# A macaron block on one core: load order of the head, state-space tables a group ahead, a higher step rate, and the last product by token halves

## The chip, the cores and the metric

The kernel runs on one core of one Trainium2 chip. The metric is device time in microseconds (us). One execution is profiled by the hardware: its span runs from the first to the last instruction of the core. TensorE is called PE in the profile, VectorE is DVE, ScalarE is ACT, GpSimd is POOL and SyncE is SP.

## The reference

One block over 256 tokens of width 2048, all in float32:

```
h = rms_norm(x);  x = x + 0.5 * (silu(h @ w_gate) * (h @ w_up)) @ w_down       # FFN1, width 5632
h = rms_norm(x);  proj = h @ w_in                                              # 1024 + 2048 columns
y_a = s5_mixer(proj[:, :1024])        # diagonal complex state space: 64 groups of 16 channels, 64 states,
                                      # x_t = a x_(t-1) + b u_t, y = gelu(Re(c x) + d u); y * sigmoid(y @ w_glu + b)
y_b = sgu_mixer(proj[:, 1024:])       # u, v = gelu halves; v = layer_norm(v); u * (w_s (masked) @ v + b_s)
g_a, g_b = sigmoid(h @ w_gate2 + b)
x = x + (g_a * (y_a @ w_branch_a) + g_b * (y_b @ w_branch_b)) @ w_out
h = rms_norm(x);  x = x + 0.5 * (silu(h @ w_gate) * (h @ w_up)) @ w_down       # FFN2
return rms_norm(x)
```

## The kernel before, in words

**Products.** Every float32 operand is split into a high part (rounded to the type fp32r) and a low part, and each product is three matmuls into one PSUM accumulator: high by high (L216), weights' low part (L217), activations' low part (L218). The tokens lie in two halves of 128 (h = 0, 1), and a matmul has 512 output columns. One `step` is one k-tile of 128 by 512 columns for both halves, six matmuls.

**Weights.** They stream through SP's DMA queue in chunks of 1 MB, 128 x 2048, that is four k-steps (24 matmuls). ScalarE makes the high part of a chunk (`whi`, L148), VectorE then the low part (`wlo`, L149). There are three raw buffers and three pairs of split buffers, and a chunk is split two chunks ahead (LOOK = 2): the split of chunk c+2 is issued at the start of chunk c and can start once chunk c-1 has been used.

**Order of the work.** The kernel writes the order of every engine's instructions by hand. `take` hands out a k-step of weights, and calls `tick` before it. A tick runs, in this order: work that was put off to this tick (`at`), evacuations of finished accumulators (`pend`), at a chunk's start the split of the chunk after next, and then steps of a filler. A filler is a generator (`s5_prepare`, `layer_norm`, `sgu`, `s5_mix`); each `yield` ends one of its steps, and each tick adds a rate (`credit[1]`: 0.3 to 0.35 in FFN1, 0.5 in the mixer) of a step. A `yield` with no work before it is a pause. `drain` runs all that is left of the fillers at once.

**Stages.** FFN1 runs in groups of 4, 4 and 3 column blocks of its hidden width, the first of them with gate and up in one pass (`begin`). In it the filler `s5_prepare` computes the tables of the state-space part and writes them to DRAM: for four groups each of `vt` (L532 to L543, from `eb` and `bt`), of `ca`, `bb` and a 64 x 64 matrix (L544 to L591, from `par`) and of `tab` (L592 to L612). Then come w_in's six jobs (v, v, ub, ub, and the two of u_a, whose evacuation writes t (L891), transposes it (L258, four transposes to a tile) and copies it to `u_all` (L883)), four pairs of a gate g_b and a branch product, three jobs of g_a, the glu product, the last g_a, the branch a, w_out, and FFN2. `sgu` (L852) runs beside the u_a jobs; `s5_mix` starts two ticks after them and is drained by `split_y` eight ticks into the third g_a job; `split_y` splits `yT` into `ysp`, which the glu product (L232) reads.

**The state-space filler.** `s5_mix` treats four groups of 8 channel pairs one after another. In each, two products with `vt` (L662) go to PSUM, VectorE rotates them by `tab` (L639), scans them (L681), rotates back into `xs`, and products with `tmat` (L698) and `cm` (L701) give y, which goes to DRAM (L713) and back in another layout (L714) on POOL's queue. `tab` and `d4` come in one buffer each, as do `tmat` and `cm`; the loads stand at the start of the group (L645 to L653).

**PSUM.** Six banks hold accumulators (three of `acc`). Two banks (pool `ms`, L91) serve all transposes, sgu products and state-space products in turn; such a tile is named q.

**The head.** Twenty small matmuls on `ident` run first. SP loads `vec_sb`, the first two tiles of the transposed input `xT`, the first chunk in four pieces, and then chunks and the rest of `xT`. `x_sb`, the input in its own layout (2 MB), is loaded through POOL's queue (L778) at tick 8, which the order of POOL places ahead of any wait.

**The end.** `down_out` runs the four column blocks m of FFN2's last group (12 k-steps, three chunks each). After the last, both halves are added to x, squared, multiplied by the norm's gain, scaled by the norm's root and stored: four pieces of 128 x 1024 on VectorE and ScalarE, 512 KB each.

## Time and profile before

| | |
|---|---|
| median of 3 runs | 2087.6 us (2086.0 to 2088.61) |
| profiled execution, device time | 2085.11 us |
| its span | 2083.3 us, 23136 instructions |
| mean granted TensorE clock | 0.991 |
| DMA | 412.20 MB, mean 198 GB/s |
| weight splits | 359 chunks; ScalarE 1.90 us, VectorE 2.27 us each (means) |

A chunk's 24 matmuls take 5.45 us, so a k-step takes 1.36. Rows of the windows table give the length of a stretch, then for PE, PEld (TensorE's weight loads), DVE, ACT and POOL the busy time and the number of instructions, then the TensorE clock granted by the throttle (1.00 is full), the share of the 16 DMA engines and GB/s. Rows of the waits give what waited and for what, then the total in us, the count and the longest. Rows of the timeline begin with the start and the length, both in us; the bracket at the end holds the engine's idle time before it and what ended it. Rows of DMA issues end with the size of one and the us from issue to landing.

### The profile page before, as it was taken

To read this page: it belongs to the slowest core of one execution; us is meant where nothing else is said; L and a number is where in the kernel's file an instruction comes from. 1 tells how busy PE (TensorE), PEld (TensorE's weight loads), DVE (VectorE), ACT (ScalarE), POOL (GpSimd) and SP (SyncE) were. 2 spreads that over 40 slices of the span, in tenths; PEclk is the share of its full clock that TensorE was granted. 3 is DMA by queue.
4 is the path that set the end of the run, shared out by engine and by line. 5 is a ranking of instruction groups with operands and counts; after the bars stand their busy time and mean duration, and the time that the engine had idled before them with its cause. 6 is when DMAs were issued, how large, how long until landed. Compare 5 with 4: busy or idle time off the path is not lost. (4 is left out here: it accounts for less than half of the span.)

```text
span 2083.3 us, 23136 instructions
## 1 busy us (share of the span) xinstructions
PE 2034.3 (98%) x9764; PEld 1681.5 (81%) x9764; DVE 1126.6 (54%) x1095; ACT 862.8 (41%) x702; POOL 73.0 (4%) x135
## 2 busy tenths in 40 slices
PE   8999999999999999999989899999999999999997
PEld 6888888887888888878777788888888888888886
DVE  4765665546664555556555665554454444544454
ACT  5543344443334454443333544443433334333443
POOL 0000001111000000011100000000000000000000
PEclk9999999999999999999999999999999999999999
DMA  7457766555655455566555455555555555555553
GB/s 305 182 197 240 244 222 210 190 201 180 221 204 195 171 191 213 191 236 211 200 200 188 170 182 182 202 198 186 191 193 191 193 184 187 194 199 185 189 180 117
DMA packets 65769, 412.20 MB, mean 198 GB/s; under 512 B 10192, under 2 KB 10592, under 8 KB 19840
## 3 DMA queue, kind: packets, MB, share of 16 engines
q1 hardware_dynamic: 52848, 376.49, 50.6%
q0 software_dynamic: 10800, 30.03, 4.5%
q10 hardware_dynamic: 2016, 4.20, 0.6%
q8 instruction: 76, 1.25, 0.2%
q14 instruction: 29, 0.24, 0.0%
HBM read 398.21 MB, written 12.45 MB: 197 GB/s over the span
## 5 line engine op out<-in xcount | busy, mean ns | idle before, releaser
L149 DVE TENSOR_TENSOR wlo<-raw,whi 128x2048 fp32r<-128x2048 f32 (+1 forms) x359 | 815.8, 2274 | 789.3 <-ACT whi L148 789.2
L148 ACT ACTIVATE whi<-raw 128x2048 fp32r<-128x2048 f32 (+1 forms) x359 | 681.5, 1901 | 907.1 <-PE acc L218 832.0
L216 PE MATMUL acc<-whi,h 128*128 128x512 f32 x1856 | 728.7, 393 | 5.9 <-ACT whi L148 5.9
L217 PE MATMUL acc<-wlo,h 128*128 128x512 f32 x1856 | 724.8, 391 | 4.8 <-DVE wlo L149 4.8
L218 PE MATMUL acc<-whi,h 128*128 128x512 f32 x1856 | 724.2, 390 | 0.0
L216 PEld LDWEIGHTS acc<-whi,h 128*128 128x128 f32 x1856 | 349.7, 188 | 79.5 <-ACT whi L148 7.0
L217 PEld LDWEIGHTS acc<-wlo,h 128*128 128x128 f32 x1856 | 349.7, 188 | 78.0 <-DVE wlo L149 6.7
L218 PEld LDWEIGHTS acc<-whi,h 128*128 128x128 f32 x1856 | 349.6, 188 | 73.2
L216 PE MATMUL acc<-whi,gt 128*128 128x512 f32 x704 | 276.0, 392 | 0.0
L218 PE MATMUL acc<-whi,gt 128*128 128x512 f32 x704 | 276.0, 392 | 0.0
L217 PE MATMUL acc<-wlo,gt 128*128 128x512 f32 x704 | 275.1, 391 | 0.0
L217 PEld LDWEIGHTS acc<-wlo,gt 128*128 128x128 f32 x704 | 132.5, 188 | 28.7
L218 PEld LDWEIGHTS acc<-whi,gt 128*128 128x128 f32 x704 | 132.6, 188 | 28.0
L216 PEld LDWEIGHTS acc<-whi,gt 128*128 128x128 f32 x704 | 132.6, 188 | 27.9
L318 ACT ACTIVATE t<-acc,rc 128x512 f32<-128x512 f32 x44 | 27.9, 686 | 69.4 <-PE acc L218 69.4
L216 PE MATMUL acc<-whi,mT 128*128 128x512 f32 x128 | 50.2, 392 | 0.0
L218 PE MATMUL acc<-whi,mT 128*128 128x512 f32 x128 | 49.8, 389 | 0.0
L217 PE MATMUL acc<-wlo,mT 128*128 128x512 f32 x128 | 49.8, 389 | 0.0
L293 DVE SCALAR_TENSOR_TENSOR x_sb<-acc,x_sb 128x1024 f32<-128x1024 f32 x27 | 33.1, 1225 | 27.6 <-PE acc L218 27.6
L273 ACT ACTIVATE junk<-x_sb 128x512 bf16<-128x512 f32 x32 | 20.2, 631 | 64.6 <-DVE x_sb L293 53.0
L328 DVE SCALAR_TENSOR_TENSOR t<-acc,rc,t 128x512 f32<-128x512 f32 x44 | 31.0, 746 | 21.7 <-PE acc L218 21.6
L244 ACT ACTIVATE gt<-q 128x512 fp32r<-128x512 f32 x44 | 23.9, 596 | 31.3 <-PE q L258 31.3
(195 smaller groups left out, 1031.2 us busy)
## 6 DMA issues: line engine op xcount, KB each, us to landing
raw<-in_w1d_dram SPq DMA_DIRECT2D x44, 1024.0 KB, 4.9
raw<-in_w2g_dram SPq DMA_DIRECT2D x44, 1024.0 KB, 4.8
raw<-in_w2u_dram SPq DMA_DIRECT2D x44, 1024.0 KB, 4.8
raw<-in_w2d_dram SPq DMA_DIRECT2D x44, 1024.0 KB, 4.8
raw<-in_w1g_dram SPq DMA_DIRECT2D x40, 1024.0 KB, 4.9
raw<-in_w1u_dram SPq DMA_DIRECT2D x40, 1024.0 KB, 4.9
raw<-in_w_in_dram SPq DMA_DIRECT2D x24, 1024.0 KB, 4.8
raw<-in_w_gb_dram SPq DMA_DIRECT2D x16, 1024.0 KB, 4.9
```

Of the source, the lines that this page charges most:

```text
L148: act.activation(out=hi[:, s], in_=r[:, s], func=AF.Copy)
L149: dve.tensor_tensor(out=lo[:, s], in0=r[:, s], in1=f(hi[:, s]), op=ALU.subtract)
L216: pe.matmul(acc[:, h, :], lhsT=lhs[:, k, 0, t], rhs=hi, start=first, stop=False)
L217: pe.matmul(acc[:, h, :], lhsT=lhs[:, k, 0, t], rhs=lo, start=False, stop=False)
L218: pe.matmul(acc[:, h, :], lhsT=lhs[:, k, 1, t], rhs=hi, start=False, stop=last)
L244: act.activation(out=dst[:, :, 0, :], in_=src, func=AF.Copy)
L273: act.activation(out=j, in_=x_sb[:, h, m * N:m * N + N], func=AF.Square, accum_out=ssq[:, h, m:m + 1])
L293: dve.scalar_tensor_tensor(out=xs, in0=acc, scalar=scale, in1=xs, op0=ALU.mult, op1=ALU.add)
L318: act.activation(out=s[:, h, :], in_=acc[:, h, :], func=AF.Silu, scale=rc(h))
L328: dve.scalar_tensor_tensor(out=s[:, h, :], in0=acc[:, h, :], scalar=rc(h), in1=s[:, h, :], op0=ALU.mult, op1=ALU.mult)
```

## The change

It has six parts. (1) In the head, `vec_sb` is loaded through ScalarE's queue; the first tile of `xT` goes alone ahead of the first piece of the first chunk, and the second tile behind that piece; `x_sb` is loaded through SP's queue between chunks, at tick 8. (2) In `s5_prepare`, `par` has two buffers and is loaded a group ahead, with its three pauses once and not per group; two more pauses stand between the load of `eb` and `bt` and their use. (3) In `s5_mix`, `tab` and `d4` of the next group are loaded after the last use of those of this group, `tmat` and `cm` after the products that read them; both stand ahead of y's transfers on POOL's queue; two more pauses precede the products. (4) Once `s5_mix` starts, the rate is 0.68 and not 0.5. (5) `sgu` has two more pauses ahead of its transposes. (6) In the last product all twelve k-steps are taken first, and then all matmuls of half 0 run, and all of half 1; each half has an epilogue of its own, in four pieces of 512 columns, with stores of 256 KB.

```diff
-    def rms():
-        r = ev.tile([P, 2], F32, tag="rc", name="rc", bufs=2)
+    def rms(hs=slice(0, 2)):
+        r = ev.tile([P, 2], F32, tag="rc", name="rc", bufs=2)[:, hs]
         s = small()
-        dve.tensor_reduce(out=s[:, 0:2], in_=ssq, axis=AX.X, op=ALU.add)
-        rsqrt(r, s[:, 0:2], D, s[:, 2:4])
+        n = hs.stop - hs.start
+        dve.tensor_reduce(out=s[:, 0:n], in_=ssq[:, hs, :], axis=AX.X, op=ALU.add)
+        rsqrt(r, s[:, 0:n], D, s[:, 2:2 + n])
...
+        def load_par(g):
+            t = pb.tile([P, 4, GP, 16], F32, tag="par", name="par", bufs=2)
+            pool.dma_start(out=t, in_=s5bc[:, :, g * GP:(g + 1) * GP, :])
+            return t
...
             yield
             yield
             yield
+            yield
+            yield
             vt = pb.tile([P, 2, GP * 64], F32, tag="p2", name="vt")
...
+        parn = load_par(0)
+        yield
+        yield
+        yield
         for g in range(NG):
             gs = slice(g * GP, (g + 1) * GP)
-            par = pb.tile([P, 4, GP, 16], F32, tag="p0", name="par")
-            pool.dma_start(out=par, in_=s5bc[:, :, gs, :])
-            yield
-            yield
-            yield
+            par = parn
+            if g + 1 < NG:
+                parn = load_par(g + 1)
...
+        def load_tab(g):
+            t = sp.tile([P, 2, GP, 64], F32, tag="tab", name="tab")
+            pool.dma_start(out=t.rearrange("p i q j -> p (i q j)"), in_=stash_w[g])
+            d = sp.tile([P, GP, 64], F32, tag="d4", name="d4")
+            act.activation(out=d, in_=rho4[:, g * GP:(g + 1) * GP].unsqueeze(2).to_broadcast([P, GP, 64]),
+                           func=AF.Copy)
+            pool.memset(d[:, :, 0:1], 0.0)
+            return t, d
+
+        def load_cm(g):
...
             o_(mt[3], mt[1], co, ALU.mult)
             o_(xs[:, 1, :, 1:65], mt[2], mt[3], ALU.add)
+            if g + 1 < NG:
+                tab, d4 = load_tab(g + 1)
+            yield
+            yield
             yield
             yield
             q = ms.tile([P, 512], F32, tag="ms", name="q")
...
+            if g + 1 < NG:
+                tmat, cm = load_cm(g + 1)
             yield
...
-    nc.sync.dma_start(out=vec_sb, in_=vec)
-    nc.sync.dma_start(out=xT[:, 0:2, :], in_=xt[:, 0:2, :])
+    act.dma_start(out=vec_sb, in_=vec)
+    nc.sync.dma_start(out=xT[:, 0:1, :], in_=xt[:, 0:1, :])
...
-    at(8, lambda: pool.dma_start(out=x_sb, in_=xk))
+    at(8, lambda: nc.sync.dma_start(out=x_sb, in_=xk))
...
             yield
             yield
+            yield
+            yield
             turned(ub, c * N, lambda b, q, c=c: split2(ybT[:, 4 * c + 2 * b:4 * c + 2 * b + 2], q))
...
+        credit[1] = 0.68
         fillers.append(s5_mix(sp, u_all))
...
-        for k in range(kt):
-            step(acc, gt, k, k == 0, k == kt - 1)
-        s = slice(3 * N, 4 * N)
+        pieces = [take(N) for _ in range(kt)]
+        c3 = slice(3 * N, 4 * N)
         for h in range(2):
-            xs = x_sb[:, h, s]
+            t = slice(h * P, h * P + P)
+            for k, (hi, lo) in enumerate(pieces):
+                pe.matmul(acc[:, h, :], lhsT=gt[:, k, 0, t], rhs=hi, start=k == 0, stop=False)
+                pe.matmul(acc[:, h, :], lhsT=gt[:, k, 0, t], rhs=lo, start=False, stop=False)
+                pe.matmul(acc[:, h, :], lhsT=gt[:, k, 1, t], rhs=hi, start=False, stop=k == kt - 1)
+            xs = x_sb[:, h, c3]
             dve.scalar_tensor_tensor(out=xs, in0=acc[:, h, :], scalar=0.5, in1=xs, op0=ALU.mult, op1=ALU.add)
             square(3, h)
-        for h in range(2):
             gained(3, h)
-        r = rms()
...
+            r = rms(slice(h, h + 1))
+            for i, eng in enumerate((dve, act, dve, act)):
+                o = xg[:, h, i * N:(i + 1) * N]
...
```

Three places show how instructions move. The first is SP's queue in the head; raw is a chunk (or a piece of 512 columns of the first one), with L143 the loader. Before:

```order
L728 DMA vec_sb<-in_vec_dram 128x56
L729 DMA xT<-in_xt_dram 128x512
L734 DMA raw<-in_w1s_dram 128x512 x4
L739 DMA xT<-in_xt_dram 128x1024
L740 DMA xT<-in_xt_dram 128x1536
L143 DMA raw<-in_w1s_dram 128x2048 x5
```

After:

```order
L754 DMA xT<-in_xt_dram 128x256
L759 DMA raw<-in_w1s_dram 128x512
L761 DMA xT<-in_xt_dram 128x256
L759 DMA raw<-in_w1s_dram 128x512 x3
L766 DMA xT<-in_xt_dram 128x1024
L767 DMA xT<-in_xt_dram 128x1536
L143 DMA raw<-in_w1s_dram 128x2048 x3
L805 DMA x_sb<-in_xk_dram 128x4096
L143 DMA raw<-in_w1s_dram 128x2048 x2
```

The first piece of the chunk moves ahead of half of the first input tiles, and x_sb, which POOL issued, now stands behind three whole chunks on SP's queue.

The second is TensorE at the first u_a evacuation, where the filler sgu runs (names with their numbers: q are tiles of the two banks of `ms`, t is the evacuated job, v and ws_sb are sgu's operands, ub its result; the bracket names the engines waited for). Before:

```order
L858 MATMUL q_5947<-v_5239,ws_sb_5237 128x128 [waits DVE_49]
L258 MATMUL q_5990<-ident_80,t_5975 128x128 [waits DVE_49,Activation_49]
L258 MATMUL q_5990<-ident_80,t_5975 128x128 [waits Activation_49]
L258 MATMUL q_5998<-ident_80,t_5975 128x128 [waits DVE_49]
L258 MATMUL q_6018<-ident_80,ub_5240 128x128 [waits DVE_49,PE_49]
L258 MATMUL q_6025<-ident_80,ub_5240 128x128 [waits DVE_49,PE_49]
```

After:

```order
L885 MATMUL q_5951<-v_5240,ws_sb_5238 128x128 [waits DVE_49]
L258 MATMUL q_5978<-ident_80,t_5963 128x128 [waits DVE_49,Activation_49]
L258 MATMUL q_5978<-ident_80,t_5963 128x128 [waits Activation_49]
L258 MATMUL q_5986<-ident_80,t_5963 128x128 [waits DVE_49,PE_49]
L885 MATMUL q_5998<-v_5240,ws_sb_5238 128x128 [waits DVE_49,PE_49]
```

Before, both sgu products of the second column half precede the transposes of t; now one precedes them and one follows. On VectorE the reader of q_5951 stands behind the copies of t's two tiles, and these behind a chunk's low part:

```order
L149 TENSOR_TENSOR wlo_5969<-raw_5883,whi_5968 128x2048 [waits DMAHW1_49,PE_49,Activation_49]
L912 COPY u_all_5234<-q_5978 128x64x4 [waits PE_49]
L912 COPY u_all_5234<-q_5978 128x64x4
L912 COPY u_all_5234<-q_5986 128x64x4 [waits PE_49]
L912 COPY u_all_5234<-q_5986 128x64x4
L891 SCALAR_TENSOR_TENSOR ub_5241<-q_5951,bs_sb_5239,ub_5241 128x128 x4
```

So q_5951 stays unread while t's two tiles and the next sgu product (q_5998) pass. Before, the reader of the last sgu product stood ahead of the low part and of the copies.

The third is POOL's queue around the second group of s5_mix. Before:

```order
L619 DMA vt<-stash_v 128x1024
L628 DMA u_6388<-u_dr 64x1x512 x2
L713 DMA y_dr<-y 4x16x512 x2
L714 DMA yT<-y_dr 32x2048
L645 DMA tab<-stash_w 128x1024
L647 DMA tmat<-stash_t 128x512
L649 DMA cm<-stash_c 128x1280
L653 MEMSET d_6660 128x8
```

After:

```order
L630 DMA vt<-stash_v 128x1024
L639 DMA u_6353<-u_dr 64x1x512 x2
L656 DMA tab<-stash_w 128x1024
L660 MEMSET d_6456 128x8
L665 DMA tmat<-stash_t 128x512
L667 DMA cm<-stash_c 128x1280
L738 DMA y_dr<-y 4x16x512 x2
L739 DMA yT<-y_dr 32x2048
```

The three table loads stand ahead of y's transfers now, and behind them before.

More of the change, by code (lines that the diff above doesn't have):

```diff
@@ L641, in s5_mix @@
         fl = lambda t: t.rearrange("p q j -> p (q j)")
+        def load_tab(g):
[7 more added lines that the diff above has]
+        def load_cm(g):
+            t = sp.tile([P, GP, 64], F32, tag="tm", name="tmat")
+            pool.dma_start(out=t.rearrange("p q c -> p (q c)"), in_=stash_t[g])
+            c = sp.tile([P, 2 * GP * 80], F32, tag="cm", name="cm")
+            pool.dma_start(out=c, in_=stash_c[g])
+            return t, c.rearrange("p (i q s) -> p i q s", i=2, q=GP)
+        tab, d4 = load_tab(0)
+        tmat, cm = load_cm(0)
+        for _ in range(7):
+            yield
         for g in range(NG):
             gs = slice(g * GP, (g + 1) * GP)
-            tab = sp.tile([P, 2, GP, 64], F32, tag="tab", name="tab")
-            pool.dma_start(out=tab.rearrange("p i q j -> p (i q j)"), in_=stash_w[g])
-            tmat = sp.tile([P, GP, 64], F32, tag="tm", name="tmat")
-            pool.dma_start(out=tmat.rearrange("p q c -> p (q c)"), in_=stash_t[g])
-            cm = sp.tile([P, 2 * GP * 80], F32, tag="cm", name="cm")
-            pool.dma_start(out=cm, in_=stash_c[g])
-            cm = cm.rearrange("p (i q s) -> p i q s", i=2, q=GP)
-            d4 = sp.tile([P, GP, 64], F32, tag="d4", name="d4")
-            act.activation(out=d4, in_=rho4[:, gs].unsqueeze(2).to_broadcast([P, GP, 64]), func=AF.Copy)
-            pool.memset(d4[:, :, 0:1], 0.0)
-            if g == 0:
-                for _ in range(7):
-                    yield
             vv = []
@@ L732 @@
     pieces = [slice(i * N, (i + 1) * N) for i in range(4)]
-    for s in pieces:
+    for i, s in enumerate(pieces):
         nc.sync.dma_start(out=r0[:, s], in_=chunks[0][:, s])
+        if i == 0:
+            nc.sync.dma_start(out=xT[:, 1:2, :], in_=xt[:, 1:2, :])
     st["load"] = 1
@@ L867, in sgu @@
             yield
+            yield
+            yield
             turned(ub, c * N, lambda b, q, c=c: split2(ybT[:, 4 * c + 2 * b:4 * c + 2 * b + 2], q))
@@ L1036, in down_out @@
         acc = new_acc()
-        for k in range(kt):
-            step(acc, gt, k, k == 0, k == kt - 1)
-        s = slice(3 * N, 4 * N)
+        pieces = [take(N) for _ in range(kt)]
+        c3 = slice(3 * N, 4 * N)
         for h in range(2):
-            xs = x_sb[:, h, s]
+            t = slice(h * P, h * P + P)
[4 more added lines that the diff above has]
+            xs = x_sb[:, h, c3]
             dve.scalar_tensor_tensor(out=xs, in0=acc[:, h, :], scalar=0.5, in1=xs, op0=ALU.mult, op1=ALU.add)
             square(3, h)
-        for h in range(2):
             gained(3, h)
-        r = rms()
-        for h, a in ((0, 0), (1, 0), (0, 1), (1, 1)):
-            s = slice(a * 1024, a * 1024 + 1024)
-            o = xg[:, h, s]
-            if h == 0:
-                dve.tensor_scalar(out=o, in0=o, scalar1=r[:, h:h + 1], scalar2=None, op0=ALU.mult)
-                nc.sync.dma_start(out=out[:, h, s], in_=o)
-            else:
-                act.activation(out=o, in_=o, func=AF.Copy, scale=r[:, h:h + 1])
-                act.dma_start(out=out[:, h, s], in_=o)
+            r = rms(slice(h, h + 1))
+            for i, eng in enumerate((dve, act, dve, act)):
+                o = xg[:, h, i * N:(i + 1) * N]
+                if eng is dve:
+                    dve.tensor_scalar(out=o, in0=o, scalar1=r, scalar2=None, op0=ALU.mult)
+                    nc.sync.dma_start(out=out[:, h, i * N:(i + 1) * N], in_=o)
+                else:
+                    act.activation(out=o, in_=o, func=AF.Copy, scale=r)
+                    act.dma_start(out=out[:, h, i * N:(i + 1) * N], in_=o)
     ffn(h3, gp2, down_out)
```

## The prediction

> **What bounds the kernel now.** I read the page's busy line first, then the windows table in steps of 10 us, then TensorE's waits, then the timeline around each wait.
>
> ```profile
> PE 2034.3 (98%) x9764; PEld 1681.5 (81%) x9764; DVE 1126.6 (54%) x1095; ACT 862.8 (41%) x702; POOL 73.0 (4%) x135
> ```
> TensorE is busy for 2034.3 of 2083.3 us. Nothing in the change removes a weight matmul, so the gain lies in the 49 us of idle time and in the time at a lower clock. The windows with idle time are these (length; busy PE, PEld, DVE, ACT, POOL; granted clock; DMA share; GB/s):
>
> ```profile
> 10.00:20.00 10.00, 6.82 (x19) 5.04 (x19) 3.48 (x6) 5.39 (x8) 0.00 (x0) 0.66 1.01 411
> 470.00:480.00 10.00, 6.04 (x24) 4.57 (x23) 9.45 (x10) 1.15 (x3) 0.55 (x1) 0.83 0.53 179
> 1010.00:1020.00 10.00, 5.00 (x54) 4.02 (x54) 5.79 (x4) 3.91 (x3) 0.00 (x0) 0.74 0.39 123
> 1060.00:1070.00 10.00, 4.60 (x52) 3.25 (x51) 9.62 (x10) 3.85 (x3) 0.00 (x0) 0.97 0.44 152
> 1110.00:1120.00 10.00, 8.88 (x37) 6.84 (x37) 9.93 (x10) 3.30 (x2) 0.00 (x0) 0.83 0.64 236
> 1150.00:1160.00 10.00, 3.08 (x13) 2.77 (x13) 8.80 (x11) 8.45 (x10) 0.00 (x0) 0.74 0.19 65
> 2070.00:2080.00 10.00, 1.17 (x6) 0.63 (x4) 4.63 (x11) 4.04 (x7) 0.00 (x0) 0.82 0.35 141
> ```
> The losses sit in the head (DMA share 1.01: the loads), in s5_prepare (470), in s5_mix (1010 to 1120), where s5_mix is drained (1150) and in the tail. The clock column gives a price: 0.83 over 10 us means 0.17 x 10 = 1.7 us lost after a wait, on top of it. I charge 1.7 us for every new wait near 3 us or more. What ends TensorE's waits (releaser: us in total, times, longest):
>
> ```profile
> PE q L701 <- DVE xs L639: 10.9, 4, 5.0
> PE acc L216 <- ACT whi L148: 5.9, 3, 4.6
> PE acc L232 <- issue: 5.4, 1, 5.4
> ```
>
> **Head.** In the timeline (start, us, engine, operation, idle before it and its releaser):
>
> ```profile
> 17.41 1.92 ACT L148 ACTIVATE whi<-raw 128x2048 fp32r<-128x2048 f32 x1 [1.62 <-DMA raw<-in_w1s_dram]
> 19.36 2.29 DVE L149 TENSOR_TENSOR wlo<-raw,whi 128x2048 fp32r<-128x2048 f32 x1 [2.96 <-ACT whi L148]
> 21.70 0.50 PE L217 MATMUL acc<-wlo,h 128*128 128x512 f32 x1 [1.48 <-DVE wlo L149]
> 5.75 0.63 ACT L148 ACTIVATE whi<-raw 128x512 fp32r<-128x512 f32 x1 [1.12 <-DMA raw<-in_w1s_dram]
> x_sb<-in_xk_dram POOLq DMA_DIRECT2D x1, 2048.0 KB, 11.1
> ```
> The second chunk lands at 17.3, and its low part is used at 21.70. Until then the queues carry 2 MB of x_sb beside it. Without x_sb the first 512 KB are there at about 5.3 (5.7 less 0.4 for vec_sb's place in the queue), and 2.10 MB more at 411 GB/s take 5.1 us: 10.4. Splitting adds 0.1 + 1.92 + 2.29: the low part is used at 14.7, 7.0 us earlier. TensorE then still waits some 3 us between the first chunk's pieces, so I charge a clock loss: -7.0 + 1.7 = **-5.3**. If the second chunk landed only at 12.3, it would be about -5.1 before the clock; without the clock loss and with vec_sb's full share, -8.0. x_sb now passes raw 6 on SP's queue; two chunks are ahead there, 10.9 us of products, against 5 us for 2 MB.
>
> **s5_prepare.**
>
> ```profile
> 467.85 1.56 DVE L380 TENSOR_TENSOR m<-an,par 128x640 f32<-128x640 f32 x2 [6.90 <-DMA par<-in_s5bc_dram]
> 471.53 0.82 DVE L380 TENSOR_TENSOR ca<-m,m 128x640 f32<-128x640 f32 x1
> 473.92 0.33 PE L258 MATMUL q<-ident,t 128*128 128x128 f32 x1 [3.63 <-DVE t L328]
> 377.38 1.07 PE L577 MATMUL q<-cas,bbs 128*16 128x64 f32 x16 [1.39 <-DVE gt L245]
> ```
> VectorE stood 6.90 us for par, and TensorE then 3.63 for an evacuation queued behind it, with two smaller waits on t (4.0 in all) and one of 1.39. With par a group ahead, 3.96 + 1.7 (clock 0.83 at 470) + 1.39 go. In the new order two chunks hold four 0.82 us products behind a low part that ends 4.3 us into a chunk: 4.3 + 3.3 = 7.6, 2.1 beyond the chunk; the next t is done at 3.5 and wanted at 2.72 (half a chunk of 5.45): 2 x 0.9 us new, bounds 0 and 2 x 2.1. Sum -7.05 + 1.8 = **-5.25**.
>
> **sgu.** This part I expect to cost.
>
> ```profile
> 884.23 2.29 DVE L149 TENSOR_TENSOR wlo<-raw,whi 128x2048 fp32r<-128x2048 f32 x1 [3.14 <-ACT whi L148]
> 886.44 1.91 DVE L883 COPY u_all<-q 128x256 f32<-128x256 f32 x4
> 882.29 1.14 PE L258 MATMUL q<-ident,t 128*128 128x128 f32 x8
> 887.61 0.63 PE L258 MATMUL q<-ident,ub 128*128 128x128 f32 x4 [1.41 <-DVE u_all L883]
> ```
> Before, eight transposes of t run back to back into two buffers. Two more yields in c=0 put the unread sgu product of c=1 into one of them when t arrives. So t's second four transposes and the next sgu product must pass through the one other buffer, each after VectorE's copies, and these stand behind the 2.29 us low part. The first four end at 882.29 + 0.57; the copies free the buffer at 887.61: TensorE stops 4.75 us in the middle of a job. The second pair of copies holds the sgu product another 1.2 us (0.63 of transposes, two copies of 0.48, less overlap). 5.95 + 1.7 of clock - 1.67 (today's waits there, 1.41 the larger) = **+5.98**. Bounds: -1.67 (no wait) and +8 (if the low part slips a further 2 us).
>
> **s5_mix.**
>
> ```profile
> 992.59 1.29 DVE L639 TENSOR_TENSOR r<-q,tab 128x512 f32<-128x512 f32 x2 [7.69 <-DMA tab<-stash_w]
> 1045.58 1.29 DVE L639 TENSOR_TENSOR r<-q,tab 128x512 f32<-128x512 f32 x2 [8.59 <-DMA tab<-stash_w]
> 1097.56 1.29 DVE L639 TENSOR_TENSOR r<-q,tab 128x512 f32<-128x512 f32 x2 [8.68 <-DMA tab<-stash_w]
> 1149.15 0.67 ACT L957 ACTIVATE ysp<-yT 128x256 fp32r<-128x256 f32 x1 [10.39 <-DMA yT<-y_dr]
> 1155.45 0.55 PE L232 MATMUL acc<-ysp,whi 128*128 128x256 f32 x1 [5.41 <-issue]
> ```
> Groups 1 to 3 each begin with VectorE 8 us late, since tab is loaded behind the y transfers on POOL's queue; TensorE pays 5.0, 5.4 (4.2 on xs, 1.2 on a low part) and 3.8 us (1.7 on xs, 1.8 and 0.2 on a chunk's two parts) and three clock losses: 14.2 + 5.1 = 19.3. The drain at the last of the mixer stops TensorE for 6.92 us (10.00 - 3.08) and costs 1.7: 8.6. The change loads tab a group ahead, and takes 75 steps at 0.68, 110 k-steps, for 67 at 0.5, 134: y is written some 24 k-steps (33 us) before split_y, three times the 10.39 that it is late. Both losses go: -27.9. New waits come with the rate:
>
> ```profile
> 922.67 0.60 POOL L619 DMA_DIRECT2D vt<-stash_v  x1
> DMA to landing us min/median/max: 7.4/7.4/7.4
> 947.33 1.28 DVE L639 TENSOR_TENSOR r<-q,tab 128x512 f32<-128x512 f32 x2
> 948.52 1.41 DVE L639 TENSOR_TENSOR r<-r,r 128x512 f32<-128x512 f32 x2
> 952.72 2.33 DVE L681 TENSOR_TENSOR_SCAN r<-d,r 128x512 f32<-128x512 f32 x2
> 980.61 1.22 DVE L935 TENSOR_TENSOR mb<-acc,mb 128x1024 f32<-128x1024 f32 x1 [1.13 <-PE acc L218]
> ```
> The first product on vt comes at 928.2 (chunk 159.75) and vt lands at 922.7 + 7.4 = 930.1: 1.9. Twice the second vt product takes the buffer that y's reader frees 5.7 us into a chunk, at 4.7: 2 x 1.0. In the last group xs is wanted four chunks, 21.8 us, after its first evacuation: 1.41 (t) + 1.06 (sigmoid) + 1.92 (high part) + 3 x 2.29 + 2.58 + 1.41 + 2.33 + 1.22 + 4.0 = 22.8, with hops 1.2 late. Sum 19.3 + 8.6 - 1.9 - 2.0 - 1.2 = **-22.8**. Bounds: -27.9 with no new wait; +14 from this if three groups miss (a rival).
>
> **Tail.**
>
> ```profile
> 2059.11 1.90 ACT L148 ACTIVATE whi<-raw 128x2048 fp32r<-128x2048 f32 x1
> 2061.04 2.29 DVE L149 TENSOR_TENSOR wlo<-raw,whi 128x2048 fp32r<-128x2048 f32 x1 [3.60 <-ACT whi L148]
> 2071.21 1.29 DVE L1042 SCALAR_TENSOR_TENSOR x_sb<-acc,x_sb 128x512 f32<-128x512 f32 x2 [7.87 <-PE acc L218]
> 2074.92 1.42 DVE L1051 TENSOR_SCALAR fin<-fin,rc 128x1024 f32<-128x1024 f32 x2
> out_dram<-fin ACTq DMA_DIRECT2D x2, 512.0 KB, 4.4
> ```
> From TensorE's end to the span's end are 12.1 us: residual, squares, gain, rms, two scalings, 2 MB out. Only one half has to follow the last matmul now, with four pieces on two engines and 1 MB: I take a third off, 8.1 (**-4.0**; bounds -2 and -6). But a half reads all three chunks in 8.2 us, where both halves took 16.35. The third is wanted 5.65 us after the product's start at 2054.85, and its high part is ready only at 2061.01, its low part at 2063.33, behind the squares and a table load on ScalarE: TensorE waits 0.75 + 2.1 = 2.85, and 1.7 of clock. Net **+0.55**.
>
> **Sum against the profiled span.** -5.3 - 5.25 + 5.98 - 22.8 + 0.55 = -26.8: a span of 2056.5, and 2058.3 with the 1.8 us outside it. The profiled execution was 2085.1, the median shown 2087.6; so 2087.6 - 26.8 = **2060.8**.
>
> **A rule against my clock price.** Row 1110 shows clock 0.83 after waits that I read as 0.22 and 1.82 us. The Trainium skill, "TensorE: Matmul & The Clock Gate", section "Part 1: The HAM clock gate (the "warmup" mystery)", has the clock fall only after a whole idle window of about 3.4 us; the row disagrees, as its waits are shorter, but the page could hold for waits spread as in the head and the tail. By that rule the sum would be 3.4 us lower.
>
> **Rivals.** *Short waits keep the clock*: the head's and the tail's waits, each about 3 us or less, cost no 1.7: 2057.4. For it: at 21.70 a wait of 1.48 was followed by a window at 1.00; against it: row 1110. Chance 0.14. *VectorE overrun*: at 0.68 each of three groups comes late by 3.0 + 1.7 us, since one chunk holds 2.29 + 4 us of steps against 5.45: +14, 2074.8. For it: VectorE was at 9.93 of 10 us at 1110; against: two extra empty steps. 0.20. *The sgu chain does not wait*: -1.67 for +5.98, 2053.1. 0.09. *The tables stay late* (the change doesn't do what it says, its loads still stuck on POOL's queue): 19.3 comes back less 3.2 of new waits that then have no cause: 2076.9. 0.05. *Slower*: the overrun carries from group to group, so that four groups stop TensorE; it decides from (27.6 + 4.5) / 4 = 8 us each. At 8.3 the time is 2094: 0.04; VectorE's 54% share speaks against it. My forecast: 0.48.
>
> **How the numbers follow.** The forecast's own range is 2054 to 2068: its bounds for the head (3), sgu (2), s5_mix (5) and the tail (2). For 8 in 10 the range reaches to the overrun and below the sgu case: 2051 to 2076. A measurement tells a difference from 0.2%, 4.2 us: faster means under 2083.4. All cases but the last are faster: 0.94; near the border 0.02; slower 0.04.
>
> **What would show it.** Right: the waits on tab and the 5.4 us "issue" wait gone; a wait of some 4.7 us on u_all near 880 less 12; the second chunk's low part at 15; a wait on wlo in the last product. Wrong: TensorE idle over 3 us per group in s5_mix, or no wait on u_all.

## The result and the profile after

The changed kernel takes 2053.7 us (median of 4 runs, 2053.59 to 2053.79) against 2087.3 us before (2086.0 to 2088.61): a ratio of 0.9839, 95% interval 0.9822 to 0.9856. On another chip the same kernel took 2054.8 us against 2085.5: 0.9854, interval 0.984 to 0.9867. The profiled execution's span is 2051.8 us, 31.5 below the 2083.3 of before; the forecast was 26.8 below.

The page's busy line and TensorE's longest waits, after (what waited, its releaser: us in total, times, longest):

```profile
PE 2027.8 (99%) x9764; PEld 1676.7 (82%) x9764; DVE 1127.6 (55%) x1102; ACT 865.0 (42%) x705; POOL 72.8 (4%) x134
```

```profile
PE q L258 <- DVE u_all L912: 4.6, 1, 4.6
PE acc L217 <- DVE wlo L149: 2.0, 2, 1.8
PE acc L1073 <- DVE wlo L149: 1.8, 1, 1.8
...
PE q L885 <- DVE u_all L912: 1.2, 1, 1.2
PE acc L216 <- ACT whi L148: 1.2, 1, 1.2
PE acc L1072 <- DVE x_sb L1076: 0.8, 1, 0.8
PE acc L1072 <- ACT whi L148: 0.8, 1, 0.8
PE q L681 <- DVE y L650: 0.7, 2, 0.4
```

The waits on xs (10.9 us before) and the 5.4 us before the glu product no longer appear. What is left stands in the three parts where the forecast expected waits: in sgu (u_all), in the head (whi, wlo) and in the last product (L1072, L1073). Only the 0.8 us on x_sb, inside the last product, were not in it. The windows that answer to those shown before, with the same columns:

```profile
10.00:20.00 10.00, 7.02 (x23) 5.17 (x22) 6.44 (x7) 5.42 (x6) 0.00 (x0) 0.83 1.01 408
470.00:480.00 10.00, 10.00 (x46) 8.19 (x45) 5.58 (x6) 5.02 (x6) 0.00 (x0) 1.00 0.48 177
870.00:880.00 10.00, 4.19 (x20) 3.21 (x19) 5.19 (x9) 2.99 (x3) 1.47 (x2) 0.79 0.42 150
880.00:890.00 10.00, 10.00 (x42) 8.29 (x42) 3.38 (x5) 1.92 (x1) 0.00 (x0) 0.87 0.11 39
1010.00:1020.00 10.00, 10.00 (x46) 8.29 (x45) 9.20 (x9) 4.58 (x3) 2.40 (x4) 1.00 0.80 220
1060.00:1070.00 10.00, 9.96 (x85) 8.10 (x84) 9.90 (x11) 4.47 (x3) 0.00 (x0) 1.00 0.50 197
1150.00:1160.00 10.00, 10.00 (x46) 8.29 (x45) 6.22 (x5) 4.79 (x4) 0.00 (x0) 1.00 0.62 217
2020.00:2030.00 10.00, 7.41 (x32) 5.62 (x31) 4.81 (x4) 4.74 (x7) 0.00 (x0) 0.97 0.00 1
2030.00:2040.00 10.00, 9.22 (x34) 7.12 (x34) 3.07 (x9) 2.47 (x5) 0.00 (x0) 0.86 0.18 69
```

All of s5_mix and its drain now run with TensorE busy and at full clock, though VectorE is at 9.90 of 10 us in one of the windows. The worst place is new: 5.81 us idle at 870, and a clock of 0.79 and 0.87.

**Where the time went, by stage.** VectorE's evacuations start right behind TensorE's jobs, so the same evacuation in both timelines dates the end of a stage. First before, then after (start, us, engine, line, operation, idle before and its releaser): the first t of FFN1 (the head's end), FFN1's last residual (s5_prepare's end), the first g_b gate (behind sgu), the last g_a gate (behind s5_mix, the drain and the glu product), and the residual of the third block of the last product (the tail's beginning).

```profile
59.99 0.75 DVE L328 SCALAR_TENSOR_TENSOR t<-acc,rc,t 128x512 f32<-128x512 f32 x1 [0.64 <-PE acc L218]
766.63 1.23 DVE L293 SCALAR_TENSOR_TENSOR x_sb<-acc,x_sb 128x1024 f32<-128x1024 f32 x1 [1.25 <-PE acc L218]
929.62 1.41 DVE L923 SCALAR_TENSOR_TENSOR t<-acc,rc,bias 128x512 f32<-128x512 f32 x2 [1.20 <-PE acc L218]
1204.29 1.41 DVE L923 SCALAR_TENSOR_TENSOR t<-acc,rc,bias 128x512 f32<-128x512 f32 x2 [1.20 <-PE acc L218]
2054.89 1.23 DVE L293 SCALAR_TENSOR_TENSOR x_sb<-acc,x_sb 128x1024 f32<-128x1024 f32 x1 [1.20 <-PE acc L218]
```

```profile
55.45 1.41 DVE L329 SCALAR_TENSOR_TENSOR t<-acc,rc,t 128x512 f32<-128x512 f32 x2 [0.65 <-PE acc L218]
756.33 1.22 DVE L294 SCALAR_TENSOR_TENSOR x_sb<-acc,x_sb 128x1024 f32<-128x1024 f32 x1 [1.25 <-PE acc L218]
927.09 1.41 DVE L953 SCALAR_TENSOR_TENSOR t<-acc,rc,bias 128x512 f32<-128x512 f32 x2 [2.51 <-PE acc L218]
1170.45 1.41 DVE L953 SCALAR_TENSOR_TENSOR t<-acc,rc,bias 128x512 f32<-128x512 f32 x2 [1.20 <-PE acc L218]
2021.19 1.23 DVE L294 SCALAR_TENSOR_TENSOR x_sb<-acc,x_sb 128x1024 f32<-128x1024 f32 x1 [1.20 <-PE acc L218]
```

| stage, up to | before | after | lead at its end | the stage itself | forecast |
|---|---|---|---|---|---|
| head | 59.99 | 55.45 | -4.5 | -4.5 | -5.3 |
| s5_prepare | 766.63 | 756.33 | -10.3 | -5.8 | -5.25 |
| sgu | 929.62 | 927.09 | -2.5 | +7.8 | +5.98 |
| s5_mix and drain | 1204.29 | 1170.45 | -33.8 | -31.3 | -22.8 |
| w_out, FFN2 | 2054.89 | 2021.19 | -33.7 | +0.1 | 0 |
| tail | 2083.3 | 2051.8 | -31.5 | +2.2 | +0.55 |

The border between sgu and s5_mix moved a little. The higher rate puts the first product of s5_mix ahead of the first g_b gate:

```profile
924.31 1.15 PE L681 MATMUL q<-u,vt 64*64 64x64 f32 x32
```

Before, it started at 933.59, behind the gate's evacuation. Some 1.3 us of sgu's +7.8 are this work (the run at rate 0.5 below has it behind the gate again), so that sgu itself cost some 6.5 us and s5_mix with its drain gained some 30.

### The profile page after: what moved, and what is told of

It reads as the page before. It is cut to its first block, busy times and chain, and to the rows that moved or that the text cites. A ratio compares the mean times of both kernels' runs of the same rounds, so it can differ in the third digit from the quotient of the medians.

```text
span 2051.8 us, 23150 instructions
## 1 busy us (share of the span) xinstructions
PE 2027.8 (99%) x9764; PEld 1676.7 (82%) x9764; DVE 1127.6 (55%) x1102; ACT 865.0 (42%) x705; POOL 72.8 (4%) x134
## 4 chain that ended last, share of the span: by engine, by line
PE 97%; DVE 1%; ACT 1%; issue 1%; DMA 0%; SPq 0%; ACTq 0%
PE acc L216 31%; PE acc L218 30%; PE acc L217 30%; PE q L258 2%; ACT whi L148 1%; PE q L588 0%; PE q L724 0%; PE acc L234 0%; PE acc L233 0%; PE acc L232 0%; DMA raw<-in_w1s_dram 0%; DVE wlo L149 0%; PE q L681 0%; PE q L885 0%; PE q L721 0%
## 5 line engine op out<-in xcount | busy, mean ns | idle before, releaser
L216 PE MATMUL acc<-whi,gt 128*128 128x512 f32 x680 | 266.1, 391 | 0.0
L218 PE MATMUL acc<-whi,gt 128*128 128x512 f32 x680 | 266.1, 391 | 0.0
L217 PE MATMUL acc<-wlo,gt 128*128 128x512 f32 x680 | 265.1, 390 | 0.0
L217 PEld LDWEIGHTS acc<-wlo,gt 128*128 128x128 f32 x680 | 127.7, 188 | 27.6
L218 PEld LDWEIGHTS acc<-whi,gt 128*128 128x128 f32 x680 | 127.7, 188 | 27.1
L216 PEld LDWEIGHTS acc<-whi,gt 128*128 128x128 f32 x680 | 127.7, 188 | 26.6
```

Source lines behind the costliest of these rows:

```text
L216: pe.matmul(acc[:, h, :], lhsT=lhs[:, k, 0, t], rhs=hi, start=first, stop=False)
L217: pe.matmul(acc[:, h, :], lhsT=lhs[:, k, 0, t], rhs=lo, start=False, stop=False)
L218: pe.matmul(acc[:, h, :], lhsT=lhs[:, k, 1, t], rhs=hi, start=False, stop=last)
```

## The experiments

All kernels below are the changed kernel with one thing undone or added; stage differences are against the changed kernel's profiled execution, read at the same evacuations. They rest on one profiled execution of each kernel, on different chips; the kernel before, run beside them, had medians of 2085.3 to 2085.7 us there.

**sgu without its two extra pauses.**

```diff
             yield
             yield
-            yield
-            yield
...
```

> The changed kernel (2053.7 us) with sgu's two extra pauses taken out and all else kept. My theory: the pauses put t's second tile and the next sgu product behind one PSUM buffer; the changed kernel shows there waits of 4.6 and 1.2 us and a lower clock (0.79 and 0.87 in two windows of 10 us, 3.4 us), where the kernel before had 1.67 us of waits. Without them 5.8 + 3.4 - 1.7 = 7.5 us go: 2046.2, and the waits on u_all fall to 1.4 and 0.3. Rival, my price of 1.7 us for the clock: 5.8 us go, 2047.9. Rival, the wait only moves (to the sgu transposes or a low part): 2051 or more.

The median is 2048.2 us, the ratio to before 0.9821 (0.9806 to 0.9836). In the trace the two waits on u_all of 4.6 and 1.2 us are replaced by the 1.7 us (two, the longest 1.4) of the kernel before, and the first g_b gate starts 6.5 us earlier. So the two pauses do cost what the buffer chain predicts, if 1 us less than the 7.5: the waits are those expected, and of the 3.4 us of clock some 2.3 show in the time (the stage is 6.4 us shorter, and the waits fall by 5.8 - 1.7 = 4.1). The span falls by 4.0 only, because the last product, which is the same program, lost more clock this time: the waits there are the same 0.8, 1.8 and 0.8 us, but the windows of this run show

```profile
2020.00:2030.00 10.00, 6.67 (x15) 4.56 (x16) 3.83 (x4) 1.51 (x4) 0.00 (x0) 0.62 0.00 0
2030.00:2040.00 10.00, 9.14 (x35) 7.08 (x33) 2.31 (x8) 1.72 (x4) 0.00 (x0) 0.87 0.28 105
```

that is 3.8 + 1.3 = 5.1 us of lost clock, where the changed kernel has 0.3 + 1.4 = 1.7 at this place. This was the first sign that the clock's price is not fixed by the wait.

**The tail as before.** The last product by k-steps with both halves, and the epilogue in four pieces of 1024 columns.

```diff
-        pieces = [take(N) for _ in range(kt)]
...
+        for k in range(kt):
+            step(acc, gt, k, k == 0, k == kt - 1)
...
         for h in range(2):
...
-            for k, (hi, lo) in enumerate(pieces):
...
```

> The changed kernel with the last product and its epilogue as before (both halves per k-step, four pieces of 1024 columns). My theory: the halves gain 3.5 us behind the last matmul (8.6 against 12.1) and lose 0.8 + 1.8 + 0.8 us of waits and about 1.6 us of clock in front of it, 5.0 to 5.7; the old tail is 1.5 to 2.2 us faster: 2051.5 to 2052.2. Rival, the waits cost only themselves and no clock: the old tail is the same or 0.1 us slower, 2053.8. Rival, the epilogue by halves is a net gain as its name says: 2057.

The median is 2053.8 us, the ratio 0.9849 (0.9835 to 0.9864), which alone tells nothing from the changed kernel. The stage does: from the third residual (2023.8) to the end (2052.1) are 28.3 us, against 30.6 in the changed kernel. The old tail is 2.3 us faster. The median does not show it; the profiled execution was already 2.6 us behind when the tail began, with more clock lost in the head (0.78 and 0.88 in two windows) and in sgu (0.79 and 0.70), and the others were not profiled. But all eight profiled executions with this tail by halves need 29.2 to 33.2 us for the stage, and the two with the old tail 28.3 and 28.4. As first written, the tail by halves is a loss. The shortest of the eight, in the ladder of waits below, lost no clock there, so the rival that the waits without a clock loss would make the two tails equal does not hold either. The last matmul's evacuation to the end is 8.6 us now and was 12.1: the 3.5 us are won, and given back with 2.3 more in front of it:

```profile
2027.34 2.29 DVE L149 TENSOR_TENSOR wlo<-raw,whi 128x2048 fp32r<-128x2048 f32 x1 [3.60 <-ACT whi L148]
2027.36 0.51 PE L1072 MATMUL acc<-whi,gt 128*128 128x512 f32 x1 [0.77 <-ACT whi L148]
2029.69 0.79 PE L1073 MATMUL acc<-wlo,gt 128*128 128x512 f32 x1 [1.82 <-DVE wlo L149]
2030.28 0.63 PE L1074 MATMUL acc<-whi,gt 128*128 128x512 f32 x1
...
2033.97 0.69 DVE L1076 SCALAR_TENSOR_TENSOR x_sb<-acc,x_sb 128x512 f32<-128x512 f32 x1 [4.34 <-PE acc L1074]
2034.72 0.50 PE L1072 MATMUL acc<-whi,gt 128*128 128x512 f32 x1 [0.78 <-DVE x_sb L1076]
```

In the timeline of the changed kernel the third chunk's parts come late (0.77 and 1.82 us, as forecast), the matmuls then go at 0.63 instead of 0.39 us, and half 1 waits another 0.78 us for the residual of half 0, though it writes the other bank: both halves are one tile, and the tile's reader is waited for.

**The rate back at 0.5, tables still a group ahead.**

```diff
-        credit[1] = 0.68
         fillers.append(s5_mix(sp, u_all))
```

> The changed kernel with the rate left at 0.5 in s5_mix, tables still loaded a group ahead. My theory: the tables no longer wait, but 75 steps at 0.5 are 150 k-steps, and there are 134 before the mixer is drained: some 8 steps (rotating back 4 us, the products, y, its activation, its way through DRAM) run in the drain. TensorE stops there for the 6.9 us of the kernel before and about 10 more, and loses 3.4 us of clock: 2053.7 + 20 = 2074; no wait on tab in groups 1 to 3. Rival, the loads a group ahead are the whole gain and the rate does nothing: 2054.

The median is 2067.7 us, the ratio 0.9916 (0.9901 to 0.9931); the profiled execution is 13.4 us behind the changed kernel, all of it in the drain. Up to the fourth branch product it is 8 us ahead of it (it has put fewer of the small products there), no group waits for tab, and at the drain TensorE waits 2.6 us for xs and 5.7 before the glu product, with a clock of 0.59 and 0.90 after it:

```profile
PE acc L232 <- issue: 5.7, 1, 5.7
...
PE q L724 <- DVE xs L650: 2.6, 1, 2.6
```

Around the drain TensorE is idle for 9.8 us, where I had expected 17, and loses 6.8 us of clock, where I had expected 3.4. The direction stands: the loads ahead alone leave the drain, and make it longer than the 6.9 us of before.

**The tables at the group's start again, rate 0.68.**

```diff
         for g in range(NG):
             gs = slice(g * GP, (g + 1) * GP)
+            tab, d4 = load_tab(g)
+            tmat, cm = load_cm(g)
...
-            if g + 1 < NG:
-                tab, d4 = load_tab(g + 1)
...
-            if g + 1 < NG:
-                tmat, cm = load_cm(g + 1)
```

> The changed kernel with tab, d4, tmat and cm loaded at the start of each group again (behind y's transfers on POOL's queue), the rate of 0.68 and the two more pauses kept. My theory: tab is 8 us late in groups 1 to 3 as before, and the 12 steps from the vt product to xs now last 24.0 us and not 27.2, so each group stops TensorE for about 8 us and loses up to 3.4 us of clock; the drain stays away: 2053.7 + 3 x 11.4 = 2088. Rival, the rate alone makes the gain (y early), the tables' lateness costs what it cost before, 19 to 24 us: 2073 to 2078. Rival, two pauses hide it: 2054 to 2060.

The median is 2064.4 us, the ratio 0.9902 (0.9886 to 0.9919); the profiled execution is 10.4 us behind the changed kernel, all of it in s5_mix. None of the sizes expected was right (2088, 2073 to 2078, 2054 to 2060). VectorE's waits on tab, in the timeline, are these:

```profile
979.68 2.48 DVE L650 TENSOR_TENSOR r<-q,tab 128x512 f32<-128x512 f32 x4 [6.98 <-DMA tab<-stash_w]
1022.06 2.48 DVE L650 TENSOR_TENSOR r<-q,tab 128x512 f32<-128x512 f32 x4 [2.60 <-DMA tab<-stash_w]
1062.58 2.49 DVE L650 TENSOR_TENSOR r<-q,tab 128x512 f32<-128x512 f32 x4 [2.29 <-DMA tab<-stash_w]
```

Only the first group is as late as before (7.69, 8.59 and 8.68 us there). In the second, tab was read 4.8 us after its issue at 1017.25 and not 7.3 (before: 1038.25 to 1045.58), and VectorE came to it behind a gate's evacuation. TensorE's waits on xs sum to 5.6 us. The loads ahead are worth some 10 us beside the higher rate, and the rate some 13 beside the loads. Alone, each brings more than half of the gain: from the first g_b gate to the last g_a gate, the loads without the rate save 16.7 us against the kernel before, the rate without the loads 21.1, and both together 31.3.

**x_sb through POOL's queue again.**

```diff
-    at(8, lambda: nc.sync.dma_start(out=x_sb, in_=xk))
+    at(8, lambda: pool.dma_start(out=x_sb, in_=xk))
```

> The changed kernel with x_sb loaded through POOL's queue again (early, beside the first chunks), the new order of SP's loads kept. My theory: the head's gain is the 2 MB that no longer share the DMA engines; the second chunk's low part is used at about 21 us again and not at 15.6, and by the first evacuation at 55.5 us the kernel is 4 us behind the changed one, with the clock of 10 to 20 us at 0.66 or 0.83. Rival, the smaller first tile and vec_sb's other queue made the gain: 0.5 us behind at most.

One execution, 2056.4 us. At the first evacuation it is 3.1 us behind (58.5 against 55.5). TensorE waits 3.5 us inside the first chunk again, for the high part of its third piece (at 12.52, as the kernel before waited 4.6 for the second), the second chunk's low part is used at 20.30, and the window from 10 to 20 us shows a clock of 0.66. So some 3 of the head's 4.5 us come from x_sb's place. That the rest is due to the order of the first loads follows by subtraction only; no run changes that order alone, and a clock step more or less moves this stage by over 1 us from one execution to the next (last section).

**s5_prepare as before.**

```diff
-            par = parn
-            if g + 1 < NG:
-                parn = load_par(g + 1)
+            par = pb.tile([P, 4, GP, 16], F32, tag="p0", name="par")
+            pool.dma_start(out=par, in_=s5bc[:, :, gs, :])
+            yield
+            yield
+            yield
```

(`load_par`, the load ahead of the loop with its three pauses, and the two pauses behind `bt` are removed as well)

> The changed kernel with s5_prepare as before (par loaded at the start of its group, no further pauses). My theory: the waits of the kernel before come back: 3.6 us on t behind the par wait, the smaller ones on t and 1.4 in front of the last tables' products, 1.7 us of clock; by the end of FFN1 (last residual, 756.3 us) it is 5.8 us behind the changed kernel, and the 0.4 us waits at 370 and 410 are gone. Rival, the new pauses cost as much as par's second buffer brings: less than 2 us behind.

One execution, 2058.3 us. From the first evacuation to FFN1's last residual it loses 5.7 us, with the old waits back (3.9 us on t, the longest 3.5, and one of 1.4 in front of the last tables' products). Its head, the same program as in the changed kernel, happened to lose no clock at all (1.00 where that shows 0.83) and was 1.6 us ahead there.

**A ladder of waits.** Eleven waits of growing length in FFN2, where nothing else disturbs TensorE.

```diff
                 s = state["g"]
+                for _ in range(late.pop(0) if late else 0):
+                    dve.tensor_tensor(out=s[:, 0, :], in0=s[:, 0, :], in1=s[:, 0, :], op=ALU.max)
...
-    ffn(h3, gp2, down_out)
+    ffn(h3, gp2, down_out, late=(3, 3, 4, 4, 5, 5, 6, 6, 8, 8, 9))
```

> The changed kernel with 3, 3, 4, 4, 5, 5, 6, 6, 8, 8 and 9 additional VectorE operations (max of a tile with itself, 0.69 us each) ahead of the eleven up evacuations of FFN2, so that TensorE's transposes come to wait for about 1, 1, 1.7, 1.7, 2.3, 2.3, 3, 3, 4.4, 4.4 and 5.1 us once in each 44.4 us. What the distance of two evacuations grows by, less the wait itself, is the price of the clock. My theory after the runs so far (losses of 1.7, 3.4 and 5.1 us): the clock is judged in windows of about 3.4 us that run freely, and a window that was idle enough costs the next at half clock; the price is 0 for waits up to 1.5 us, 0 or 1.7 by chance for 1.7 to 3, and 1.7 or 3.4 for over 4 us, in steps of 1.7. Rival, the price of my prediction: 1.7 for each wait of about 3 us or more and nothing else. Rival, it grows with the wait: half of it or so, no steps.

One execution, 2077.3 us. The waits came out shorter than planned, since there was more room ahead of the transposes. From 0.88 us on each wait in the table is the sum of two, with one transpose between them (3.05 is 2.72 + 0.33). "Growth" is by how much two gates' evacuations stand further apart than in the changed kernel (for the last, up to the next residual).

| operations | TensorE's waits (us) | growth (us) | growth less wait | clock of the windows |
|---|---|---|---|---|
| 3, 3 | none | 0, 0 | 0 | 1.00 |
| 4, 4 | 0.33, 0.33 | 0.55, 0.57 | 0.2 | 1.00 |
| 5, 5 | 0.88, 0.87 | 1.32, 1.27 | 0.4 | 1.00 |
| 6, 6 | 1.60, 1.59 | 2.01, 2.01 | 0.4 | 1.00 |
| 8 | 3.05 | 5.10 | 2.0 | 0.83 |
| 8 | 2.89 | 6.04 | 3.1 | 0.70, 0.96 |
| 9 | 3.63 | 6.8 | 3.2 | 0.76, 0.90 |

The windows around the last three (waits at 1895.07, 1944.60 and 1995.83):

```profile
1890.00:1900.00 10.00, 6.95 (x28) 5.36 (x27) 8.78 (x11) 2.78 (x3) 0.00 (x0) 0.83 0.33 115
1940.00:1950.00 10.00, 7.10 (x25) 5.48 (x24) 8.33 (x11) 2.32 (x3) 0.00 (x0) 0.70 0.37 130
1950.00:1960.00 10.00, 10.00 (x44) 8.23 (x43) 3.28 (x2) 3.83 (x2) 0.00 (x0) 0.96 0.44 171
1990.00:2000.00 10.00, 6.37 (x24) 4.96 (x23) 9.52 (x12) 2.81 (x3) 0.00 (x0) 0.76 0.28 98
2000.00:2010.00 10.00, 10.00 (x41) 8.11 (x41) 2.29 (x1) 3.62 (x2) 0.00 (x0) 0.90 0.42 155
```

0.17 x 10 = 1.7; 3.0 + 0.4 = 3.4; 2.4 + 1.0 = 3.4. Here waits up to 1.6 us cost no clock; at 3 us two waits of nearly the same length cost one step of 1.7 us and two. The steps hold, and the price is not in proportion to the wait; that 2.9 us can already cost two steps I had not expected. In the time the two steps show as 2.7 to 2.8 us, if the 0.4 of the rows without a clock loss is taken off. My flat 1.7 is the lower step.

The same execution has a result that I had not looked for. In its last product TensorE waits 0.77, 1.82 and 0.78 us as in the changed kernel, but the windows from 2050 to 2070 us show a clock of 1.00: no step at all, and the stage is 1.4 us shorter than there (29.2 against 30.6).

**Repairs of sgu and the last product.** Two pauses for sgu's first half and four for the second, the third chunk's split ahead of the third block's evacuation, a PSUM tile for each half.

```diff
-            yield
-            yield
-            yield
-            yield
+            for _ in range(2 + 2 * c):
+                yield
...
+        split_to(st["sub"] + LOOK)
         acc = new_acc()
         pieces = [take(N) for _ in range(kt)]
...
+            if h == 1:
+                acc = new_acc()
```

> The changed kernel with three repairs: sgu pauses 2 times for its first column half and 4 times for the second; ahead of the last product the split of its third chunk is issued before the evacuation of the block before it; and the two halves accumulate in different PSUM tiles. My theory: sgu's waits go altogether (6.5 us as in the run with the old pauses, and the 1.7 us that are left there), and the last product has no waits (0.8 + 1.8 + 0.8) and no clock loss (1.6): 2053.7 - 8.2 - 5.0 = 2040.5. Rival, the third chunk's split now delays the squares and the residual, and the epilogue ends later by 2 us: 2042.5. Rival, the wait on the third chunk is set by its load, not by the order on ScalarE: 2043.9.

2039.6 us (2039.51 to 2041.25), ratio 0.9785 (0.9768 to 0.9801). The first g_b gate is 8.0 us earlier, and from the second block's residual to the end are 41.2 us (1996.7 to 2037.9) instead of 46.9 (2004.9 to 2051.8): 5.7 more. The kernel before takes 44.7 there (2038.57 to 2083.3), so the tail by halves, with its two repairs, does gain 3.5 us. Neither sgu nor the last product shows a wait or a clock loss. The third block's residual does start later now (by 4.2 us relative to the rest), and nothing waits for it.

**The same with a repaired head, beside both others on one chip.** The second chunk in four pieces, xT's last six tiles behind the fourth chunk.

```diff
-        load_to(i)
...
+    r1 = wp.tile([P, SUB], F32, tag="raw", name="raw", bufs=NRAW)
+    for s in pieces:
+        nc.sync.dma_start(out=r1[:, s], in_=chunks[1][:, s])
...
-    nc.sync.dma_start(out=xT[:, 10:16, :], in_=xt[:, 10:16, :])
...
-    split_to(1)
+    load_to(3)
+    nc.sync.dma_start(out=xT[:, 10:16, :], in_=xt[:, 10:16, :])
...
+    for s in pieces:
+        split_piece(hi1, lo1, r1, s)
```

> The changed kernel itself, beside the two repaired ones on one chip. Expected against the kernel before: a ratio of 0.984 (0.9822 to 0.9856), and a spread of some 2 to 4 us between runs if the clock's price depends on where its windows fall (steps of 1.7 us), under 0.5 us if the price is fixed.

> The kernel with sgu's and the last product's repairs, again. Expected: 13 to 14 us under the changed kernel; since only the head's wait can still cost clock, runs differ by one or two steps of 1.7 us at most.

> As the run before, and in the head the second chunk is loaded and split in four pieces, and the last six tiles of xT are loaded behind the fourth chunk. My theory: the waits of 1.6 us (high part) and 1.8 us (low part) on the second chunk go, and with them a clock loss of 1.7 us; the third chunk is then late by up to 1 us: 3 to 5 us under the run before. Rival, the head is bound by the bytes (408 to 420 GB/s) and the wait moves to the third or fourth chunk: within 1 us of the run before.

| kernel | median (us) | runs | ratio to before |
|---|---|---|---|
| before | 2085.5 | 2083.04 to 2086.92 | |
| changed | 2054.8 | 2054.08 to 2055.83 | 0.9854 (0.984 to 0.9867) |
| with sgu and tail repaired | 2039.8 | 2039.44 to 2041.31 | 0.9782 (0.9768 to 0.9795) |
| and the head | 2037.6 | 2036.37 to 2038.37 | 0.977 (0.9757 to 0.9784) |

The repairs are worth 15.0 us, a little over the 13 to 14 expected. The head's brings 2.2 and not 3 to 5: the second chunk no longer waits, but the third one does, as its rival half said, and the 1.7 us of clock are lost behind it:

```profile
19.42 0.50 PE L217 MATMUL acc<-wlo,h 128*128 128x512 f32 x1 [1.82 <-DVE wlo L149]
20.00:30.00 10.00, 10.00 (x38) 8.07 (x37) 8.59 (x10) 7.90 (x11) 0.00 (x0) 0.83 1.01 422
```

This wait stands alone: between 7 and 19 us TensorE waits for nothing else. So a single wait of 1.82 us can cost a whole step.

The changed kernel's runs spread over 1.75 us, one step, and not the 2 to 4 expected.

## Why the prediction was right or wrong

All four signs of being right came: the waits on tab and the 5.4 us before the glu product are gone, a wait of 4.6 us on u_all stands at 876, the second chunk's low part is used at 15.64, and the last product waits for wlo.

**Head, -5.3, measured -4.5: right in what the early chunk brings, but the wait stood elsewhere.** The second chunk's low part is used at 15.64 instead of 21.70; I had 14.7. I had put a wait of some 3 us between the first chunk's pieces, and charged a clock step for it. Inside the first chunk no wait is longer than 0.3 us; the 3 us stand at the second chunk (1.15 us for its high part, 1.82 for its low part), and the step follows them. That the sum of the waits and the step fit is luck.

```profile
11.35 1.91 ACT L148 ACTIVATE whi<-raw 128x2048 fp32r<-128x2048 f32 x1 [1.60 <-DMA raw<-in_w1s_dram]
13.32 0.50 PE L216 MATMUL acc<-whi,h 128*128 128x512 f32 x1 [1.15 <-ACT whi L148]
15.64 0.80 PE L217 MATMUL acc<-wlo,h 128*128 128x512 f32 x1 [1.82 <-DVE wlo L149]
```

The chunk landed at 11.3, not 10.4. The run with x_sb on POOL gives some 3 of the 4.5 to x_sb.

**s5_prepare, -5.25, measured -5.8: right.** The new waits I charged with 1.8 us are 0.7 (two of 0.33 on t), where I had said two of 0.9. The run with the old s5_prepare returns 5.7.

**sgu, +5.98, measured +7.8, of which sgu itself some 6.5: right in mechanism, the clock somewhat too cheap.** The timeline has the two waits of the forecast (4.75 and 1.2) almost to the tenth:

```profile
873.02 2.29 DVE L149 TENSOR_TENSOR wlo<-raw,whi 128x2048 fp32r<-128x2048 f32 x1 [5.14 <-ACT whi L148]
875.23 1.02 DVE L912 COPY u_all<-q 128x256 f32<-128x256 f32 x2
876.40 1.09 PE L258 MATMUL q<-ident,t 128*128 128x128 f32 x4 [4.60 <-DVE u_all L912]
877.52 1.02 DVE L912 COPY u_all<-q 128x256 f32<-128x256 f32 x2 [1.27 <-PE q L258]
878.69 2.04 PE L885 MATMUL q<-v,ws_sb 128*128 128x128 f32 x8 [1.21 <-DVE u_all L912]
```

The clock there lost 3.4 us (2.1 + 1.3 in the two windows), two steps and not one; some 2.3 of them show in the time, against the 1.7 charged. The other 1.3 us of the stage are the product that moved in from s5_mix.

**s5_mix, -22.8, measured -31.3 (some -30 without the product that moved to sgu's stage): right in direction, two terms mis-sized.** First, "three clock losses" and the drain's, 4 x 1.7 = 6.8: the windows of before hold 10.2 (2.6 + 0.8 behind group 1, 0.3 + 1.4 behind group 2, 1.7, and 2.6 + 0.8 behind the drain). I had quoted 0.74 for 1010 and for 1150, and charged 1.7 for what that row and the next priced at 3.4. These are the next rows, of the kernel before:

```profile
1020.00:1030.00 10.00, 10.00 (x83) 7.87 (x83) 3.27 (x2) 3.20 (x2) 0.00 (x0) 0.92 0.21 88
1070.00:1080.00 10.00, 10.00 (x91) 8.16 (x89) 2.29 (x2) 2.13 (x2) 0.00 (x0) 0.86 0.42 165
1160.00:1170.00 10.00, 10.00 (x80) 10.00 (x79) 5.26 (x7) 6.14 (x6) 0.00 (x0) 0.92 0.70 256
```

Second, the new waits of 5.1 us: 0.7 came. vt landed 4.0 us after its issue at 918.40, where I had taken 7.4, and no product waited for it; the second vt products waited 0.7 in all, not 2.0; the last xs was just in time, not 1.2 late, because the scans started at 1058.13, half a microsecond ahead of my sum. The two terms make 3.4 + 4.4 us, and the product that moved 1.3: 9.1, against a difference of 8.5. The 0.6 us left over are not placed; not all of a clock loss shows in the time (last section).

**Tail, +0.55, measured +2.2: the sign was right, and two terms were missed.** The waits on the third chunk are as worked out (0.77 + 1.82 against 0.75 + 2.1). The epilogue won 3.5, not 4.0. What I did not see is the 0.8 us for which half 1 waits for the reader of half 0, since both are one tile, and that a stop costs more than its wait: in the ladder's execution, whose clock stays at 1.00 here, the first half takes 3.2 us longer than in the repaired kernel for 2.6 us of waits, some 0.3 for each stop. The first half of the changed kernel takes 1.45 us longer than the ladder's; that is the clock, forecast as 1.7. So 3.4 of waits + 0.9 of stops + 1.45 of clock - 3.5 of epilogue make the +2.2.

**Rivals.** The higher rate did not overrun VectorE: TensorE's waits in s5_mix sum to 0.7 us. The rule that short waits keep the clock fell in the changed kernel: the head's and the tail's waits of 1.15 + 1.82 and 0.77 + 1.82 us each cost a step. But my flat price does not hold either: in two other executions (the head with the old s5_prepare, the last product of the ladder) the same sort of waits cost nothing, and in a third (the last product without sgu's pauses) three steps. The sgu chain waited; the tables came in time. The slower case had no footing.

**The total**, -26.8, measured -31.5: the gain is larger than forecast by the mis-sized s5_mix (8.5), less what sgu, the tail and the head cost more (1.8 + 1.7 + 0.8), with 0.5 from s5_prepare. By the medians the gain is 33.6; I had taken 2087.6 as the start, and the profiled execution, from whose rows the sum comes, was 2.5 us faster than that. So the forecast of 2060.8 is 7.1 too high: 4.7 by the terms, the rest by the start. The time of 2053.7 lies in the wide range (2051 to 2076) and just under the forecast's own (2054 to 2068). That it does is in part luck: the range reached below 2054 for the case that the sgu chain does not wait, which was priced at 2053.1. The sgu chain did wait, and what came on top of the forecast is s5_mix's.

## What to carry to other kernels

Price a lost clock from the row of the place itself and the next one, as one number per place and not one number for all, and from more than one execution: here it came in steps of 1.7 us, from none to three, at one and the same place. When a schedule moves work between two users of a small buffer pool, check which tile is still unread as the next ones pass; two more pauses for each half here cost some 6.5 us, and with two for the first half and four for the second that came back, and the 1.7 us of waits of the kernel before with it. A split of a product into two passes halves the time that the last weight chunk has to arrive, so its preparation must move ahead by as much.
